# Feed-forward weights in steps of 1024 elements, in slots that stay through the whole kernel

## The chip, the cores and the metric

The kernel runs on one core of a Trainium2 chip. The metric is the device time of one execution in microseconds (us). Before the change the median of 3 runs is 1696.09 us (1696.07 to 1696.68).

## The reference

One layer of a streaming encoder on x of 256 rows (SEQ) by 2048 (D), all float32:

```
h      = RMSNorm(x) * attn_norm_g
proj   = h @ w_in                       # latents, rope key, diff q/k/v, gate logits
y_mla  = latent attention (16 heads),  y_diff = differential attention (8 heads)
merged = g0 * (y_mla @ w_mla_proj) + g1 * (y_diff @ w_diff_proj)
x      = x + merged @ w_out
h2     = RMSNorm(x) * ffn_norm_g
x      = x + (silu(h2 @ w_gate) * (h2 @ w_up)) @ w_down     # 2048 -> 5632 -> 2048
out    = RMSNorm(x) * final_norm_g
```

The change lies in the feed-forward part (the last three lines) and in the slots for weights that the part before it, here called the front, uses too.

## The kernel before

**Precision.** Every product of two float32 matrices is made of three matmuls. `split` (L89 to L97) makes of a tile a high part (ACT's cast to fp32r, L92) and a low part (DVE's difference of the tile and its high part, L93). `mm3` (L174 to L178) issues left high x right high (L176), left high x right low (L177) and left low x right high (L178) into one PSUM bank. The left operand is a 128x128 block of activations that TensorE loads, the right one a weight block of 128x512 that it streams. So each weight is loaded, cast by ACT, subtracted by DVE and then used by TensorE.

**Front (up to 945 us).** `weights` (L134) loads tiles of up to 128 x 2 x 512 into `raw` (6 slots of 4 KB a partition), high parts into `whi`, low parts into `wlo` (4 slots each). `project` and `project_t` use them; attention runs in between as generators that `advance` steps. All these slots lie in the pool `wp`, which is closed at the end of the front with the attention's pool `ap` and the front's PSUM pool `ps` (`front.close()`). The last product of the front is `w_out` (L586 to L607): its result plus x gives x2 (L593), which TensorE transposes (L601); ACT and DVE scale and split it (L95, L96) into `h2T`, 16 blocks of 128 x 256.

**Feed-forward.** Behind it two pools are opened, `fp` (SBUF) and `fq` (PSUM), on the memory that the front has left; each tile waits for the old tiles under it. `fp` holds `raw` (3 slots of 128 x 4 x 512, 8 KB a partition), `w` (5 such slots, for high and low parts and for sums) and `r` (2 slots of 128 x 3 x 512).

The 5632 hidden columns are 11 blocks of 512, in three `parts` of 4, 4 and 3. For each part `hidden(c, ...)` makes its blocks one after the other, and then the down projection adds their share to x2, in four column groups c of 512.

In `hidden` the 16 blocks of `h2T` go in 8 pairs. A pair needs four weight blocks from `w_gu`: u0, g0 (up and gate for the first block of the pair) and u1, g1 (for the second); one load of 1 MB brings them. A plain pair makes 2 halves of rows x 2 blocks x (gate, up) = 8 products, 24 matmuls, into the banks 2, 3, 4 and 8. Pairs 0, 2 and 4 (`SEVEN`) are done as a 2x2 block product by seven products, 21 matmuls, into banks 1 to 7. Their right sides are three loaded blocks (g0, g1, u1; parts in `r`) and four sums: T1 = g0 + u0, T3 = u1 + u0 (both L638), T2 = T1 + u1 (L639), T4 = T2 + g1 (L640); parts in `w`. The left sides are blocks of `h2T` and sums of them made in the front (`h2S`). Behind pair 4, DVE and ACT gather banks 1, 5, 6, 7 (L690 to L694); behind pair 7 they empty banks 2, 3, 4 and 8 and make silu(gate) * up (L714, L715, L717, L718). The result is transposed before pair 6 of the next block, or in the down projection (L668).

In the down projection each load of `w_fd` brings four blocks of 128 x 512 (a step m): 4 x 2 products, 24 matmuls; L753 adds a group's result to x2. The last column group of the last part has its weights split ahead into `L` tiles and is normalized and stored at once.

**Order.** Each engine runs its instructions in the order of the instruction stream. That order is set when the kernel is built: a scheduler goes through the program in order of priority (program order first) with estimated times and gives each engine, at each estimated moment, the first instruction that is ready and whose tiles have a slot. So instructions of later steps can stand ahead of earlier ones that were estimated to wait, on TensorE too. All weight loads are issued on SP's queue, each when a `raw` slot is free.

Of the kernel before, what the change touches and what calls it, by code (L numbers as in the profile page):

```python
# [8 lines left out]
F32 = mybir.dt.float32  # L9
# [5 lines left out]
P = 128  # L15
# [23 lines left out]
def hybrid_block(ctx: ExitStack, tc: tile.TileContext, x, xT, gains, w_lat, w_kr, w_dqk, w_dv, w_g0, w_g1, b_gate,  # L39
# [4 lines left out]
    up = ctx.enter_context(tc.tile_pool(name="up", bufs=1))  # L44
    st = ctx.enter_context(tc.tile_pool(name="st", bufs=1))
    dram = ctx.enter_context(tc.tile_pool(name="dram", bufs=1, space=bass.MemoryType.DRAM))

    front = ExitStack()
    wp = front.enter_context(tc.tile_pool(name="wp", bufs=1))
    ap = front.enter_context(tc.tile_pool(name="ap", bufs=1))  # L50
    ps = front.enter_context(tc.tile_pool(name="ps", bufs=1, space=bass.MemoryType.PSUM))

# [81 lines left out]
    def weights(w, c, g0=0, ng=None, cut=None, alloc=None):  # L134

        m, n = w.shape[3:]
        cut = cut or m
        full = [P, 1024 // n, n] if n == 256 else [P, 2, 512]
        res = []
        for g in range(g0, g0 + (ng or w.shape[1])):  # L140
            raw = wp.tile([P, m, n], F32, tag="raw", name=nm("raw"), bufs=6, padded_shape=full)
            if alloc is None:
                for i in range(0, m, cut):
                    nc.sync.dma_start(out=raw[:, i:i + cut], in_=w[c, g, :, i:i + cut])
                whi = wp.tile([P, m, n], F32R, tag="whi", name=nm("whi"), bufs=4, padded_shape=full)
                wlo = wp.tile([P, m, n], F32R, tag="wlo", name=nm("wlo"), bufs=4, padded_shape=full)
            else:
                nc.sync.dma_start(out=raw, in_=w[c, g])
            for i in range(0, m, cut):
                if alloc is None:  # L150
                    hi, lo = whi[:, i:i + cut], wlo[:, i:i + cut]
                else:
                    hi, lo = alloc(F32R, (P, cut, n)), alloc(F32R, (P, cut, n))
                split(raw[:, i:i + cut], hi, lo)
                res += [(hi[:, j], lo[:, j]) for j in range(cut)]
        return res
# [315 lines left out]
    t1 = []  # L472
# [147 lines left out]
        return fq.tile(list(shape), F32, tag=f"q{role}", name=nm("q"), bufs=1)  # L620

    def load(src):
        raw = fp.tile([P, 4, 512], F32, tag="raw", name=nm("raw"), bufs=3)
        nc.sync.dma_start(out=raw, in_=src)
        return raw

    def wide(dt=F32R):
        return fp.tile([P, 4, 512], dt, tag="w", name=nm("w"), bufs=5)

    def plain_weights(src):  # L630
        raw, hi, lo = load(src), wide(), wide()
        split(raw, hi, lo)
        return [(hi[:, j], lo[:, j]) for j in range(4)]

    def seven_weights(src):

        raw, t = load(src), wide(F32)
        nc.vector.tensor_tensor(out=t[:, 0:2], in0=raw[:, 1::2], in1=raw[:, 0:1].broadcast_to([P, 2, 512]), op=ALU.add)  # L638
        nc.vector.tensor_tensor(out=t[:, 2], in0=t[:, 0], in1=raw[:, 3], op=ALU.add)  # L639
        nc.vector.tensor_tensor(out=t[:, 3], in0=t[:, 2], in1=raw[:, 2], op=ALU.add)  # L640
        rh, rl = (fp.tile([P, 3, 512], F32R, tag="r", name=nm("r"), bufs=2) for _ in range(2))
        split(raw[:, 1:4], rh, rl)
        th, tl = wide(), wide()
        split(t, th, tl)
        return [(rh[:, j], rl[:, j]) for j in range(3)], [(th[:, j], tl[:, j]) for j in range(4)]

    def part_of(a, h):
        hs = slice(h * P, (h + 1) * P)
# [1 line left out]

    def seven_products(q, pair, w, start, stop):

        (b11, b21, b22), (t1, t3, t2, t4) = w
        hi, lo = h2S[pair]
        s1, s3, s2, s4 = [(hi[:, j], lo[:, j]) for j in range(4)]
        a0, a1 = h2T[2 * pair], h2T[2 * pair + 1]
        for i, l, r in ((1, part_of(a0, 0), b11), (5, s1, t1), (7, s3, t3), (6, s2, t2),
                        (2, part_of(a1, 0), b21), (3, s4, b22), (4, part_of(a1, 1), t4)):
            mm3(q[i], l, r, start, stop and i in (1, 5, 6, 7))

    def transposed(f, alloc=lt, roles=(5, 6)):

# [12 lines left out]
    def hidden(c, between):  # L675

        pairs = len(h2T) // 2
        last = max(SEVEN) if SEVEN else None
        q, base = {}, None
        for p in range(pairs):  # L680
            if p == pairs - 2:
                between()
            if p in SEVEN:
                w = seven_weights(w_gu[c, p])
                if not q:
                    q = {i: bank(i) for i in (1, 5, 7, 6, 2, 3, 4)}
                seven_products(q, p, w, p == min(SEVEN), p == last)
                if p == last:
                    c1, v2, v3, d12, d22 = (sc() for _ in range(5))
                    nc.scalar.copy(c1, q[1])  # L690
                    nc.vector.tensor_tensor(out=v2, in0=c1, in1=q[6], op=ALU.add)
                    nc.vector.tensor_tensor(out=d12, in0=q[5], in1=v2, op=ALU.subtract)
                    nc.vector.tensor_tensor(out=v3, in0=q[7], in1=v2, op=ALU.add)
                    nc.vector.tensor_tensor(out=d22, in0=q[5], in1=v3, op=ALU.subtract)  # L694
                    base = ((c1, d12), (v3, d22))
                continue
            u0, g0_, g1_, u1 = plain_weights(w_gu[c, p])
            if 8 not in q:
                q[8] = bank(8)
            if not SEVEN and not p:  # L700
                q.update({i: bank(i) for i in (2, 3, 4)})
            for a, (wg, wu) in ((h2T[2 * p], (g0_, u0)), (h2T[2 * p + 1], (g1_, u1))):
                first_k = a is h2T[0]
                for h, (i, j) in enumerate(((2, 3), (4, 8))):
                    l = part_of(a, h)
                    end = a is h2T[-1]
                    mm3(q[i], l, wg, first_k, end)
                    mm3(q[j], l, wu, first_k or (j == 8 and SEVEN and p == 1 and a is h2T[2]), end)
        f = []
        for h, (i, j) in enumerate(((2, 3), (4, 8))):  # L710
            sg = nt()
            gate, up_ = q[i], q[j]
            if base:
                nc.vector.tensor_tensor(out=sg, in0=base[h][0], in1=gate, op=ALU.add)  # L714
                nc.vector.tensor_tensor(out=base[h][1], in0=base[h][1], in1=up_, op=ALU.add)  # L715
                gate, up_ = sg, base[h][1]
            nc.scalar.activation(out=sg, in_=gate, func=AF.Silu, scale=r2[:, h:h + 1])  # L717
            nc.vector.scalar_tensor_tensor(out=sg, in0=up_, scalar=r2[:, h:h + 1], in1=sg, op0=ALU.mult, op1=ALU.mult)  # L718
            f.append(sg)
        return f  # L720
# [42 lines left out]
        nc.gpsimd.tensor_scalar(out=rest[:, h:h + 1], in0=s3, scalar1=D * EPS, scalar2=None, op0=ALU.add)  # L763
    ws = []
    for m in range(a, b):
        raw = load(w_fd[3, m])
        for j in range(4):
            ws.append((lt(F32R, (P, 512)), lt(F32R, (P, 512))))
            split(raw[:, j], ws[-1][0], ws[-1][1])
    for h in range(2):  # L770
        hs = slice(h * P, (h + 1) * P)
        z, y = x2[3][h], lt(shape=(P, 512))
# [56 lines left out]
def _arrays(inputs):  # L829

    import numpy as np

    a = {n: np.asarray(v) for n, v in inputs.items()}
    a["xT"] = a["x"][0].T.reshape(D // P, P, S).transpose(1, 0, 2)
    a["gains"] = np.concatenate([a[n][0].reshape(-1, P).T for n in
                                 ("attn_norm_g", "ffn_norm_g", "q_norm_g", "kv_norm_g")], axis=1)
    w = a["w_in"][0]
    a["w_lat"], a["w_kr"] = _tiles(w[:, :1024], 512), _tiles(w[:, 1024:O_DQ], 320)
    a["w_dqk"], a["w_dv"] = _tiles(w[:, O_DQ:O_DV], 256), _tiles(w[:, O_DV:O_G], 512)
    a["w_g0"], a["w_g1"] = _tiles(w[:, O_G:O_G + D], 256), _tiles(w[:, O_G + D:], 512)  # L840
    w = a["w_uq"][0].reshape(QR, NH, QK)
    a["w_qn"] = _tiles(w[:, :, :NOPE].reshape(QR, -1), 256)
    a["w_qr"] = _tiles(w[:, :, NOPE:].reshape(QR, -1), 512)
    w = a["w_ukv"][0].reshape(KVR, NH, NOPE + VD)
    a["w_kn"] = _tiles(w[:, :, :NOPE].reshape(KVR, -1), 256)
    a["w_v"] = _tiles(w[:, :, NOPE:].reshape(KVR, -1), 256)
    for n, src, cols in (("w_mla", "w_mla_proj", 512), ("w_diff", "w_diff_proj", 512), ("w_out", "w_out", 512)):
        a[n] = _tiles(a[src][0], cols)

    wg, wu = (a[n][0].reshape(D // (2 * P), 2, P, NF, 512).transpose(3, 0, 1, 2, 4)  # L850
              for n in ("w_ffn_gate", "w_ffn_up"))
    a["w_gu"] = np.stack([wu[:, :, 0], wg[:, :, 0], wg[:, :, 1], wu[:, :, 1]], axis=3)
    a["w_fd"] = a["w_ffn_down"][0].reshape(NF, 4, P, 4, 512).transpose(3, 0, 2, 1, 4)
    a["consts"] = _constants()
    return [(n, np.ascontiguousarray(a[n])) for n in _INS]
# [16 lines left out]
```

## Time and profile before

| | |
|---|---|
| Median of 3 runs | 1696.09 us |
| Profiled execution, own time | 1696.72 us |
| Its span in the profile | 1694.9 us |
| Mean granted TensorE clock | 0.997 |
| TensorE matmuls | 1659.5 us busy, 98% of the span, 8443 matmuls |
| TensorE weight loads | 1405.4 us, 83% |
| DVE (VectorE) | 1146.8 us, 68% |
| ACT (ScalarE) | 829.2 us, 49% |
| GpSimd | 27.5 us, 2% |
| Mean DMA rate | 191 GB/s, 323.61 MB in all |

Busy times are those of one execution, taken by the hardware profiler. Matmuls are pipelined and their ends are modelled: the busy time of TensorE contains overlaps, and the idle time shown before a matmul is counted from the modelled end of the one before it. Lines such as L93 are lines of the kernel; `w<-raw,w` means that tile `w` is written from tiles `raw` and `w`.

### The profile page before, as it was taken

The numbers are of one execution on the slowest core, as the hardware profiler recorded it, in microseconds if no ns is written. First come the engines' busy times: TensorE is split into PE (matmuls) and PEld (weight loads), VectorE is DVE, ScalarE is ACT, GpSimd is POOL, SyncE is SP. The second block draws the span as 40 slices with busy tenths as digits, with TensorE's granted clock in tenths as the row PEclk, the third lists the DMA queues.
The fourth block names the chain that finished last, engine by engine and source line by source line (L and its number), as shares of the span: only waits on it lengthen the run. The fifth ranks groups of instructions, "written<-read, shape, count | busy, mean of one in ns | idle before, by whom it ended". The sixth has DMA issues, their size and how long they took to land.

```text
span 1694.9 us, 21463 instructions
## 1 busy us (share of the span) xinstructions
PE 1659.5 (98%) x8443; PEld 1405.4 (83%) x8443; DVE 1146.8 (68%) x1328; ACT 829.2 (49%) x998; POOL 27.5 (2%) x49
## 2 busy tenths in 40 slices
PE   8999999999999999999999899999999999999998
PEld 6888888888888999998888677787887777887776
DVE  7676666665545766665566688874688874588765
ACT  6455454544444665664444355543355553345532
POOL 0000000010000000000000000000000000000010
PEclk9999999999999999999999999999999999999999
DMA  9655455465665554456655455554555554555553
GB/s 324 217 174 174 174 175 180 146 205 201 217 207 190 175 175 166 160 191 223 233 201 199 142 180 199 199 199 174 183 201 189 197 199 174 200 198 197 185 195 118
DMA packets 80118, 323.61 MB, mean 191 GB/s; under 512 B 8848, under 2 KB 14992, under 8 KB 63120
## 3 DMA queue, kind: packets, MB, share of 16 engines
q1 hardware_dynamic: 79872, 322.21, 54.7%
q8 instruction: 66, 1.08, 0.3%
q14 instruction: 36, 0.29, 0.1%
q10 hardware_dynamic: 144, 0.02, 0.0%
HBM read 315.91 MB, written 6.29 MB: 190 GB/s over the span
## 4 chain that ended last, share of the span: by engine, by line
PE 88%; DVE 7%; issue 2%; ACT 2%; DMA 0%; SPq 0%; ACTq 0%; POOL 0%; POOLq 0%; DVEq 0%
PE mm L177 12%; PE mm L176 12%; PE mm L178 12%; PE q L177 11%; PE q L178 11%; PE q L176 10%; PE mm L201 9%; PE mm L202 5%; DVE w L93 3%; DVE r L93 2%; ACT w L92 2%; PE ps L178 1%; PE ps L177 1%; PE ps L176 1%; DVE n L718 1%
## 5 line engine op out<-in xcount | busy, mean ns | idle before, releaser
L93 DVE TENSOR_TENSOR wlo<-raw,whi 128x1024 fp32r<-128x1024 f32 (+3 forms) x320 | 381.8, 1193 | 266.2 <-ACT whi L92 260.0
L92 ACT CAST whi<-raw 128x1024 fp32r<-128x1024 f32 (+3 forms) x320 | 328.9, 1028 | 347.9 <-PE mm L178 221.6
L176 PE MATMUL mm<-whi,L 128*128 128x512 f32 (+2 forms) x1080 | 385.3, 359 | 5.4 <-ACT whi L92 5.4
L177 PE MATMUL mm<-wlo,L 128*128 128x512 f32 (+2 forms) x1080 | 386.0, 358 | 0.5 <-DVE wlo L93 0.5
L178 PE MATMUL mm<-whi,L 128*128 128x512 f32 (+2 forms) x1080 | 384.8, 357 | 0.0
L177 PE MATMUL q<-w,L 128*128 128x512 f32 x900 | 353.6, 393 | 11.6 <-DVE w L93 11.5
L178 PE MATMUL q<-w,L 128*128 128x512 f32 x900 | 351.0, 391 | 0.0
L176 PE MATMUL q<-w,L 128*128 128x512 f32 x900 | 308.8, 391 | 0.8 <-ACT w L92 0.7
L92 ACT CAST w<-raw 128x2048 fp32r<-128x2048 f32 x96 | 183.3, 1914 | 173.5 <-PE q L178 108.2
L93 DVE TENSOR_TENSOR w<-raw,w 128x2048 fp32r<-128x2048 f32 x96 | 219.6, 2288 | 57.5 <-PE q L177 38.0
L201 PE MATMUL mm<-L,whi 128*128 128x512 f32 x672 | 239.6, 398 | 0.6 <-DVE n L211 0.6
L176 PEld LDWEIGHTS mm<-whi,L 128*128 128x128 f32 x1080 | 204.1, 189 | 33.8 <-ACT whi L92 5.9
L177 PEld LDWEIGHTS mm<-wlo,L 128*128 128x128 f32 x1080 | 204.1, 189 | 28.9 <-DVE wlo L93 1.5
L178 PEld LDWEIGHTS mm<-whi,L 128*128 128x128 f32 x1080 | 204.0, 189 | 28.3
L177 PEld LDWEIGHTS q<-w,L 128*128 128x128 f32 x900 | 168.9, 188 | 54.8 <-DVE w L93 19.8
L176 PEld LDWEIGHTS q<-w,L 128*128 128x128 f32 x900 | 168.2, 188 | 36.1 <-ACT w L92 2.0
L178 PEld LDWEIGHTS q<-w,L 128*128 128x128 f32 x900 | 169.0, 188 | 34.0
L202 PE MATMUL mm<-L,wlo 128*128 128x256 f32 x672 | 189.2, 282 | 0.0
L201 PEld LDWEIGHTS mm<-L,whi 128*128 128x128 f32 x672 | 126.2, 188 | 28.7 <-DVE n L211 0.9
L202 PEld LDWEIGHTS mm<-L,wlo 128*128 128x128 f32 x672 | 127.0, 189 | 0.6
L92 ACT CAST w<-w 128x2048 fp32r<-128x2048 f32 x33 | 63.0, 1910 | 112.9 <-DVE w L640 98.6
L93 DVE TENSOR_TENSOR w<-w,w 128x2048 fp32r<-128x2048 f32 x33 | 75.6, 2292 | 59.7 <-ACT w L92 55.6
(190 smaller groups left out, 1364.8 us busy)
## 6 DMA issues: line engine op xcount, KB each, us to landing
raw<-in_w_gu_dram SPq DMA_DIRECT2D x88, 1024.0 KB, 4.7
raw<-in_w_fd_dram SPq DMA_DIRECT2D x44, 1024.0 KB, 4.7
raw<-in_w_dqk_dram SPq DMA_DIRECT2D x64, 512.0 KB, 4.0
raw<-in_w_g_dram SPq DMA_DIRECT2D x64, 512.0 KB, 3.3
raw<-in_w_diff_dram SPq DMA_DIRECT2D x32, 512.0 KB, 3.3
raw<-in_w_mla_dram SPq DMA_DIRECT2D x32, 512.0 KB, 4.2
raw<-in_w_out_dram SPq DMA_DIRECT2D x32, 512.0 KB, 3.9
raw<-in_w_dv_dram SPq DMA_DIRECT2D x30, 512.0 KB, 3.2
```

Of the source, the lines that this page charges most:

```text
L92: nc.scalar.copy(hi, src)
L93: nc.vector.tensor_tensor(out=lo, in0=src, in1=hi.bitcast(F32), op=ALU.subtract)
L176: nc.tensor.matmul(o, lhsT=l[0], rhs=r[0], start=start, stop=False)
L177: nc.tensor.matmul(o, lhsT=l[0], rhs=r[1], start=False, stop=False)
L178: nc.tensor.matmul(o, lhsT=l[1], rhs=r[0], start=False, stop=stop)
L201: nc.tensor.matmul(o[b], lhsT=ws[k][0][:, bs], rhs=a, start=k == 0, stop=False)
L202: nc.tensor.matmul(o[b][:, :S], lhsT=ws[k][1][:, bs], rhs=ah, start=False, stop=k == len(aT) - 1)
L718: nc.vector.scalar_tensor_tensor(out=sg, in0=up_, scalar=r2[:, h:h + 1], in1=sg, op0=ALU.mult, op1=ALU.mult)
```

## The change

Weights of the feed-forward part move to the pool `wp`, which now stays open to the end of the kernel, in `raw` (6 slots) and `w` (8 slots), each of 128 x 2 x 512 (4 KB a partition). The front's `whi` and `wlo` become tiles of this `w`. Each load of 128 x 4 x 512 becomes two of 128 x 2 x 512, and each high or low part is made for 2 blocks at once. For a pair by seven products the sums and the parts of the loaded blocks go into five slots `t` of the pool `fp`; the parts of the sums go into `w`. The order of the four blocks in `w_gu` (set when the arrays are laid out on the host) becomes g0, u1, u0, g1, so that T1 and T3 are one sum of the first half with u0. In the second and third pair by seven products of a block, the products of loaded blocks (1, 3, 2) come first; in the first pair the order of products stays.

```diff
@@ pools
+    wp = ctx.enter_context(tc.tile_pool(name="wp", bufs=1))
     front = ExitStack()
-    wp = front.enter_context(tc.tile_pool(name="wp", bufs=1))
@@ weights()
-                whi = wp.tile([P, m, n], F32R, tag="whi", name=nm("whi"), bufs=4, padded_shape=full)
-                wlo = wp.tile([P, m, n], F32R, tag="wlo", name=nm("wlo"), bufs=4, padded_shape=full)
+                whi = wp.tile([P, m, n], F32R, tag="w", name=nm("whi"), bufs=8, padded_shape=full)
+                wlo = wp.tile([P, m, n], F32R, tag="w", name=nm("wlo"), bufs=8, padded_shape=full)
@@ feed-forward helpers
     def load(src):
-        raw = fp.tile([P, 4, 512], F32, tag="raw", name=nm("raw"), bufs=3)
+        raw = wp.tile([P, 2, 512], F32, tag="raw", name=nm("raw"), bufs=6)
         nc.sync.dma_start(out=raw, in_=src)
         return raw

-    def wide(dt=F32R):
-        return fp.tile([P, 4, 512], dt, tag="w", name=nm("w"), bufs=5)
+    def two():
+        return wp.tile([P, 2, 512], F32R, tag="w", name=nm("w"), bufs=8)
+
+    def extra(dt=F32R):
+        return fp.tile([P, 2, 512], dt, tag="t", name=nm("t"), bufs=5)
+
+    def parts_of(src, alloc):
+        hi, lo = alloc(), alloc()
+        split(src, hi, lo)
+        return [(hi[:, j], lo[:, j]) for j in range(2)]

     def plain_weights(src):
-        raw, hi, lo = load(src), wide(), wide()
-        split(raw, hi, lo)
-        return [(hi[:, j], lo[:, j]) for j in range(4)]
+        return [w for m in (0, 2) for w in parts_of(load(src[:, m:m + 2]), two)]

     def seven_weights(src):
-        raw, t = load(src), wide(F32)
-        nc.vector.tensor_tensor(out=t[:, 0:2], in0=raw[:, 1::2], in1=raw[:, 0:1].broadcast_to([P, 2, 512]), op=ALU.add)
-        nc.vector.tensor_tensor(out=t[:, 2], in0=t[:, 0], in1=raw[:, 3], op=ALU.add)
-        nc.vector.tensor_tensor(out=t[:, 3], in0=t[:, 2], in1=raw[:, 2], op=ALU.add)
-        rh, rl = (fp.tile([P, 3, 512], F32R, tag="r", name=nm("r"), bufs=2) for _ in range(2))
-        split(raw[:, 1:4], rh, rl)
-        th, tl = wide(), wide()
-        split(t, th, tl)
-        return [(rh[:, j], rl[:, j]) for j in range(3)], [(th[:, j], tl[:, j]) for j in range(4)]
+        a, b = load(src[:, 0:2]), load(src[:, 2:4])
+        t13, t24 = extra(F32), extra(F32)
+        nc.vector.tensor_tensor(out=t13, in0=a, in1=b[:, 0:1].broadcast_to([P, 2, 512]), op=ALU.add)
+        nc.vector.tensor_tensor(out=t24[:, 0], in0=t13[:, 0], in1=a[:, 1], op=ALU.add)
+        nc.vector.tensor_tensor(out=t24[:, 1], in0=t24[:, 0], in1=b[:, 1], op=ALU.add)
+        w = {}
+        w[1], w[3] = parts_of(a, extra)
+        b21 = extra()
+        split(b[:, 1], b21[:, 0], b21[:, 1])
+        w[2] = b21[:, 0], b21[:, 1]
+        w[5], w[7] = parts_of(t13, two)
+        w[6], w[4] = parts_of(t24, two)
+        return w
@@ seven_products()
-        for i, l, r in ((1, part_of(a0, 0), b11), (5, s1, t1), (7, s3, t3), (6, s2, t2),
-                        (2, part_of(a1, 0), b21), (3, s4, b22), (4, part_of(a1, 1), t4)):
-            mm3(q[i], l, r, start, stop and i in (1, 5, 6, 7))
+        ls = {1: part_of(a0, 0), 2: part_of(a1, 0), 3: s4, 4: part_of(a1, 1), 5: s1, 6: s2, 7: s3}
+        for i in (1, 5, 7, 6, 2, 3, 4) if start else (1, 3, 2, 5, 7, 6, 4):
+            mm3(q[i], ls[i], w[i], start, stop and i in (1, 5, 6, 7))
@@ hidden()
-            u0, g0_, g1_, u1 = plain_weights(w_gu[c, p])
+            g0_, u1, u0, g1_ = plain_weights(w_gu[c, p])
@@ last column group
-        raw = load(w_fd[3, m])
         for j in range(4):
+            if j % 2 == 0:
+                raw = load(w_fd[3, m][:, j:j + 2])
             ws.append((lt(F32R, (P, 512)), lt(F32R, (P, 512))))
-            split(raw[:, j], ws[-1][0], ws[-1][1])
+            split(raw[:, j % 2], ws[-1][0], ws[-1][1])
@@ arrays on the host
-    a["w_gu"] = np.stack([wu[:, :, 0], wg[:, :, 0], wg[:, :, 1], wu[:, :, 1]], axis=3)
+    a["w_gu"] = np.stack([wg[:, :, 0], wu[:, :, 1], wu[:, :, 0], wg[:, :, 1]], axis=3)
```

## Rows read from the trace of the kernel before

**Rows 1.** Busy table of the whole span: busy us, share, instructions.

```profile
PE 1659.5 (98%) x8443; PEld 1405.4 (83%) x8443; DVE 1146.8 (68%) x1328; ACT 829.2 (49%) x998; POOL 27.5 (2%) x49
```

**Rows 2.** Timeline of TensorE: start us, us from first start to last end, instructions, [idle before].

```profile
968.04 1.75 PE L176 MATMUL q<-w,L 128*128 128x512 f32 x7
...
1143.00 0.38 PE L668 MATMUL q<-ident,n 128*128 128x128 f32 x2
...
1148.26 0.60 PE L668 MATMUL q<-ident,n 128*128 128x128 f32 x4
...
1150.63 0.50 PE L177 MATMUL q<-w,L 128*128 128x512 f32 x1 [1.30 <-DVE w L93]
...
1320.49 1.07 PE L176 MATMUL q<-w,L 128*128 128x512 f32 x4
1322.04 0.50 PE L176 MATMUL q<-r,L 128*128 128x512 f32 x1 [0.48 <-ACT r L92]
```

**Rows 3.** TensorE's waits before 945 us: in total, times, longest us.

```profile
PE mm L176 <- ACT whi L92: 5.4, 2, 4.5
```

**Rows 4.** TensorE's waits from 945 us on.

```profile
PE q L177 <- DVE w L93: 11.5, 17, 1.3
PE q L176 <- ACT r L92: 7.6, 9, 4.0
```

**Rows 5.** Stretches: length, busy us (instructions) of PE, PEld, DVE, ACT, POOL, clock, DMA.

```profile
945.50:965.00 19.50, 14.11 (x50) 9.65 (x50) 16.53 (x21) 8.70 (x9) 1.07 (x3) 0.82 0.26 83
1308.25:1352.20 43.95, 43.07 (x192) 34.98 (x191) 37.82 (x33) 22.53 (x17) 0.00 (x0) 1.00 0.54 191
1142.50:1164.00 21.50, 19.02 (x85) 15.05 (x85) 9.84 (x8) 8.07 (x6) 0.00 (x0) 1.00 0.33 117
1222.00:1264.00 42.00, 42.00 (x187) 34.75 (x186) 34.58 (x27) 19.37 (x12) 0.00 (x0) 1.00 0.58 200
...
951.30:958.10 6.80, 6.19 (x14) 3.78 (x14) 4.83 (x5) 4.19 (x4) 0.00 (x0) 0.62 0.46 154
```

**Rows 6.** Timeline of DVE, ACT and TensorE at the entry of the feed-forward part.

```profile
945.02 1.37 DVE L593 TENSOR_TENSOR L<-n,mm 128x512 f32<-128x512 f32 x2 [7.45 <-PE mm L178]
...
947.03 0.47 ACT L95 ACTIVATE L<-ps,gT 128x256 fp32r<-128x256 f32 x1 [10.74 <-PE ps L601]
...
949.84 1.46 ACT L92 CAST r<-raw 128x1536 fp32r<-128x1536 f32 x1
...
951.36 1.65 PE L176 MATMUL q<-r,L 128*128 128x512 f32 x3 [4.04 <-ACT r L92]
```

**Rows 7.** Timeline of DVE at the boundary of two blocks.

```profile
1310.17 2.29 DVE L93 TENSOR_TENSOR w<-raw,w 128x2048 fp32r<-128x2048 f32 x1
1312.38 1.22 DVE L638 TENSOR_TENSOR w<-raw 128x1024 f32<-128x1024 f32 x1
1313.51 1.41 DVE L718 SCALAR_TENSOR_TENSOR n<-s,r,n 128x512 f32<-128x512 f32 x2
...
1319.96 2.29 DVE L93 TENSOR_TENSOR w<-w,w 128x2048 fp32r<-128x2048 f32 x1 [2.05 <-ACT w L92]
```

**Rows 8.** Groups of instructions by shape: busy us, mean ns of one, idle before.

```profile
L93 DVE TENSOR_TENSOR wlo<-raw,whi 128x1024 fp32r<-128x1024 f32 x292 | 357.1, 1223 | 240.1 <-ACT whi L92 234.0 <-PE ps L514 3.5 <-DMA raw<-in_w_mla_dram 1.5
L93 DVE TENSOR_TENSOR w<-raw,w 128x2048 fp32r<-128x2048 f32 x96 | 219.6, 2288 | 57.5 <-PE q L177 38.0 <-issue 12.9 <-PE q L178 3.5
L92 ACT CAST whi<-raw 128x1024 fp32r<-128x1024 f32 x292 | 307.2, 1052 | 316.1 <-PE mm L178 205.4 <-PE mm L201 44.0 <-issue 32.2
L93 DVE TENSOR_TENSOR r<-raw,r 128x1536 fp32r<-128x1536 f32 x33 | 57.8, 1751 | 3.9 <-ACT r L92 3.9
L639 DVE TENSOR_TENSOR w<-w,raw 128x512 f32<-128x512 f32 x33 | 22.6, 686 | 0.4
```

**Rows 9.** DMA issues: tile, count, KB each, median us from issue to landing.

```profile
raw<-in_w_gu_dram SPq DMA_DIRECT2D x88, 1024.0 KB, 4.7
...
raw<-in_w_dqk_dram SPq DMA_DIRECT2D x64, 512.0 KB, 4.0
raw<-in_w_g_dram SPq DMA_DIRECT2D x64, 512.0 KB, 3.3
```

More of the change, by code (lines that the diff above doesn't have):

```diff
@@ L651, in seven_products @@
     def seven_products(q, pair, w, start, stop):
-        (b11, b21, b22), (t1, t3, t2, t4) = w
         hi, lo = h2S[pair]
```

## The prediction

> **What bounds the kernel now.** I read the busy table first. It shows TensorE's matmul row at 98% [rows 1], but the length of a matmul there is modelled and matmuls overlap, so 98% does not say how much is lost. The distance from one matmul to the next does. A run of seven takes 1.75 us and a run of four 1.07 us, so a matmul of 512 columns costs (1.75 - 1.07) / 3 = 0.227 us; a 128-column transpose costs (0.60 - 0.38) / 2 = 0.11 us [rows 2]. Second I read who TensorE waited for. In the whole front (up to 945 us) its largest wait is 5.4 us, 4.5 of it one wait at the start of the kernel [rows 3]. Almost all else is in the feed-forward part: `q` matmuls waiting for DVE's `w` (17 times) and for ACT's `r` (9 times) [rows 4]. So the kernel is bound by TensorE's issue, and what can be won are the holes of the feed-forward part. The weights made by ACT (cast) and DVE (subtraction) come too late there.
>
> Third I sized the holes by stretches [rows 5], as length minus matmuls times spacing:
> - **Entry, 945.5 to 965**: 50 matmuls, 8 of them transposes. 42 x 0.227 + 8 x 0.11 = 10.4 us of work in 19.5: 9.1 us lost. In its middle the granted clock is 0.62 of full, a mix of the 2.4 and 1.2 GHz levels, after TensorE had been nearly idle.
> - **A block of `hidden` that follows another block, 1308.25 to 1352.2**: 3 x 21 + 5 x 24 = 183 matmuls and 8 transposes, 42.4 us of work in 43.95: 1.6 us lost. The 9 waits for `r` [rows 4] are one at the entry and eight such blocks: 8 x 1.6 = 12.8 us.
> - **A block that follows the down projection, 1222 to 1264**: 187 matmuls in 42.0 us with TensorE busy throughout; nothing lost. So pairs by seven products are not in themselves too dear for DVE.
> - **The start of a down projection, 1142.5 to 1164**: 77 + 8 matmuls, 18.4 us of work in 21.5: 3.1 us lost, three times (one for each entry of `parts`): 9.3 us.
>
> Together 31 us, 1.8% of the profiled execution's 1696.72 us. That is all the change can win, since it takes no matmul away: a pair by seven products keeps 21, a plain pair 24.
>
> **The change part by part.**
>
> *Slots kept through the kernel (entry).* Before the entry DVE sits idle 7.45 us and ACT 10.74 us [rows 6], though only TensorE's last products of `w_out` keep them from feed-forward weights: the new pool lies on the memory of the front's weights, so `t`, `r` and `w` come free as those do. The first `r` is cast at 949.84, and TensorE starts at 951.36. With `raw` and `w` kept and `t` on the memory of the attention's pool (long unused), the first pair's sums, its loaded halves and then T1 to T4 can be made while `w_out` still runs: sums 1.22 + 2 x 0.69, subtractions 3 x 1.22 + 0.69, some 6.9 us [rows 8], which fits the 7.45 us that DVE was idle. The first four products need banks that the front's `mm` tiles have left, so TensorE can start when the last transposes are issued, or before. The clock also has no long pause in which to fall. Of 9.1 us I take 8 as gained. Bounds: 0 (the order is as before and DVE gets to it late) to 9.
>
> *Steps of 1024 elements.* One subtraction of 2048 elements takes 2.29 us, two of 1024 take 2 x 1.22 = 2.45: +0.16. A pair by seven products had 1.22 + 2 x 0.69 for its sums and 1.75 + 2.29 for its subtractions, 6.64 us; it now has the same sums, three subtractions of 1.22 and one of 0.69: 6.95, +0.31 [rows 8]. So DVE's work in one block rises by 3 x 0.31 + 5 x 0.16 = 1.7 us, from 37.8 [rows 5] to 39.5 us, against 42.4 us of TensorE work. By starts instead of durations it is less: the sum of 1024 at 1312.38 is followed at 1313.51 [rows 7], 1.13 us and not 1.22. This costs TensorE nothing while DVE is below it, but the cover is thin: 2.9 us in a block. The Trainium skill ("Perfetto Trace Analysis", Optimizing Scalar/DVE Operations) gives about 60 ns of fixed access cost per DVE instruction on SBUF and advises grouping where the engine is saturated. Eleven more instructions would by that be about 0.7 us a block, an estimate from that page; the rows above give up to 1.7, and the sum goes by the rows. The same section says that breaking up instructions helps where an unsaturated engine makes bubbles elsewhere, and the next paragraph is where that must show.
>
> *Loaded blocks first (boundary of two blocks).* At 1310.0 DVE is through the four sums that empty the old block's banks. Before, it then made one plain subtraction (from 1310.17), the sum, two L718, `r`, two more sums, waited 2.05 us for the cast of the whole `w`, and subtracted until 1322.25 [rows 7]; the products of T waited for that, and the next pair's `r` with them [rows 2]. After, from 1310.0 by starts: plain 2 x 1.13, T1/T3 1.13, L718 1.33, T2 and T4 1.4, the half `a` 1.13 (done 1317.3), g1 0.7 (1318.0), T1/T3 1.13 (1319.1), T2/T4 1.2 (1320.3). TensorE reaches this pair at 1318.45 and does products 1, 3, 2 first, 9 x 0.227 = 2.04 us; it wants `a`'s low parts from 1318.7, g1's at about 1320.0, T1's at 1320.7 and T2's at 1322.1. Everything is ready 1.4 us or more ahead. ACT has no single cast of 1.9 us left in this chain: while DVE sums, it casts what is there, so the 2.05 us wait goes. The plain pair behind has its subtractions from 1320.3 to 1322.6 and is wanted at 1323.4: this is late next, with 0.8 us to spare. I take 10 of 12.8 us as gained; bounds 0 to 12.8, and below nothing if DVE becomes the bound (rivals).
>
> *Down projection.* A half step's slots come free 12 matmuls (2.7 us) before the step ends, and a half's subtraction takes 1.2 us instead of 2.29. The hole of 1.3 us before the low products at 1150.63 [rows 2] should mostly close: 7 of 9.3 us; bounds 0 to 9.3.
>
> *Loads.* 132 loads of 1 MB become 264 of 512 KB. The front already lives on 512 KB loads that land in 3.3 to 4.0 us against 4.7 for 1 MB [rows 9], one each 2.7 us of TensorE work, without TensorE waiting [rows 3]. Cost nothing. SP issues 132 more; behind them stand only the final gains and the stores. The front's whi and wlo now share eight slots instead of four each: taken as 0, bounds -1 to +15 us (a rival has it).
>
> *Sum.* 8 + 10 + 7 = 25 us: 1696.72 - 25 = 1671.7 for a profiled execution; the median of the runs shown is 0.6 us under it, so **1671 us**.
>
> **The rivals.**
>
> *DVE becomes the bound in the blocks.* For it: 39.5 us of busy time, and if the 5.5 us or so of waits for casts stay (2.05 us [rows 7] in most of three pairs), 45 us against 43.95 now. The boundaries then gain nothing or lose 1 us each (8 us), while entry and down projection still gain 15: 1682 to 1690. Against it: the casts no longer come in one piece behind the last sum.
>
> *The gains cancel* with new holes of the same size: 1693 to 1699.
>
> *Casts take the slots (slower).* Eight slots under one name serve high and low parts. If a cast of the next step takes a slot before the subtraction it precedes, that low part waits until the running pair ends, because in a plain gate/up pair both halves ([g0, u1], [u0, g1]) are read to the end. u0's low part is wanted 4 matmuls, 0.91 us, into the pair; made after the slot is free it is there after 1.22 us, or 1.05 + 1.22 = 2.27 if the cast is late too [rows 8]: 0.3 to 1.4 us in each of 55 plain pairs, 17 to 75 us, against 15 from the other places: 1698 to 1756, say 1715. It decides from 0.27 us a pair on. Against it: at the boundary the writers of the shared `w` slots come in the order of the program (plain, sums, T) [rows 7].
>
> *The halves of a load come one after the other.* Then 1 MB takes 2 x 3.3 = 6.6 us or more [rows 9] against 24 x 0.227 = 5.4 of TensorE: 132 x 1.2 = 158 us slower, 1830. Against it the front, where such loads overlap. The Trainium skill ("DMA: Bandwidth & Descriptors", Measured) asks for batches of 1 MiB or more and so speaks against the change; the trace does not bear it out, since TensorE waits for none of the 512 KB loads behind the start [rows 3].
>
> **How the numbers follow.** Forecast (1664 to 1681) 0.66; DVE bound 0.18; cancelled 0.05; slots 0.09; loads 0.02. Faster by over 0.2% (3.4 us, about what a measurement of this kernel can tell from no change) 0.84, within 0.05, slower 0.11. The range reaches from all 31 us and a little more won to the end of the second case: 1663 to 1690.
>
> **What would show it.** Right: no pause between the last `w_out` transposes and the first product of the entry, and granted clock 1.0 there; TensorE's waits for `r`/`t` and `w` down from some 20 us to under 6; a block after a block in 42.4 to 42.8 us; DVE's wait for ACT at T gone. Wrong: DVE at 40 us or more in a block with TensorE waiting for low parts (first rival); a short hole before the low products of every plain pair (slots); waits for `raw` (loads); or holes in the front, where now there are none.

## The result, and the profile after

The changed kernel takes 1665.55 us (median of 4 runs, 1665.15 to 1666.32) against 1696.38 us for the kernel before on the same chip: a ratio of 0.9818, 95% interval 0.9801 to 0.9835. That is 30.8 us, where 25 were forecast (1671 us, range 1663 to 1690). The span of the profiled execution fell from 1694.9 to 1663.6 us.

The waits of TensorE from 945 us on (each line: total us, times, longest us) are the first view, and the answer to [rows 4]: both kinds of wait for weights are gone, and what is left is three short waits at the entry, 2.3 us in all.

```profile
PE ps L601 <- DVE L L593: 2.0, 2, 1.8
PE q L176 <- DVE L L96: 0.3, 1, 0.3
```

The stretches of [rows 5], found by counting matmuls from the start, in the same order (length, then busy us and instructions of PE, PEld, DVE, ACT, POOL, granted clock, DMA share, GB/s):

```profile
944.81:958.00 13.19, 10.90 (x50) 8.54 (x50) 11.62 (x19) 6.19 (x9) 1.07 (x3) 1.00 0.36 117
1289.66:1331.88 42.22, 42.22 (x191) 34.94 (x190) 37.83 (x44) 23.22 (x28) 0.00 (x0) 1.00 0.62 199
1128.68:1147.03 18.35, 18.35 (x85) 15.25 (x84) 10.18 (x11) 8.32 (x9) 0.00 (x0) 1.00 0.56 186
1205.06:1246.99 41.93, 41.93 (x186) 34.72 (x185) 33.54 (x36) 20.45 (x23) 0.00 (x0) 1.00 0.62 199
```

The second one starts one matmul (0.23 us) later than the stretch of [rows 5]. Before the change the stretch between the same two matmuls reads:

```profile
1308.47:1352.21 43.74, 42.86 (x191) 34.79 (x190) 37.61 (x33) 22.32 (x17) 0.00 (x0) 1.00 0.54 192
```

The entry went from 19.50 to 13.19 us (-6.3, forecast -8), this block that follows a block from 43.74 to 42.22 (-1.5), the start of a down projection from 21.50 to 18.35 (-3.15). Counted in the same way at every place, the eight blocks that follow a block gained 1.5 to 2.4 us each, 14.0 together (forecast 10), the three down projections 9.0 (forecast 7), and the rest of the first block 1.0. That is 30.3 of the 31.3 us by which the profiled span fell; the remaining 1.0 lies before the entry and at the end. The fourth stretch, without a hole before, moved by 0.07. In both middle stretches PE's busy time equals the length: TensorE is at its spacing of 0.227 us and nothing is left there.

At the boundary of two blocks DVE's timeline reads (answers to [rows 7]; the new block's first matmul starts at 1289.44):

```profile
1292.77 2.35 DVE L93 TENSOR_TENSOR w<-raw,w 128x1024 fp32r<-128x1024 f32 x2
...
1295.71 1.21 DVE L93 TENSOR_TENSOR w<-t,w 128x1024 fp32r<-128x1024 f32 x1
1296.84 1.22 DVE L93 TENSOR_TENSOR t<-raw,t 128x1024 fp32r<-128x1024 f32 x1
1297.98 1.22 DVE L93 TENSOR_TENSOR w<-t,w 128x1024 fp32r<-128x1024 f32 x1
1299.11 0.68 DVE L93 TENSOR_TENSOR t<-raw,t 128x512 fp32r<-128x512 f32 x1
```

The low parts of T1 and T3 are done at 1296.9, those of T2 and T4 at 1299.2, the last loaded one at 1299.8. TensorE reaches this pair at 1299.6 (45 matmuls, 10.2 us, behind the block's first) and issues its first matmul with the low part of a loaded block at 1302.1. No row has a wait for a cast in front.

At the entry the rest shows:

```profile
946.07 1.27 DVE L593 TENSOR_TENSOR L<-n,mm 128x512 f32<-128x512 f32 x2
...
946.80 0.44 PE L601 MATMUL ps<-ident,L 128*128 128x128 f32 x2 [1.83 <-DVE L L593]
...
948.03 0.47 PE L176 MATMUL q<-t,L 128*128 128x512 f32 x1
```

The first product follows the last transpose directly (0.6 us from 947.39 to 948.03 for six of them) and the granted clock of the stretch is 1.00. But L593, which ran as soon as `w_out` was through [rows 6], now starts 1.1 us after it: a subtraction for the plain pair (L93, from 944.33) and a sum (L647, from 945.46) stand ahead of it on DVE.

### The profile page after: what moved, and what is told of

Its sections match the earlier page's. It is cut to its first block, busy times and chain, and to the rows that moved or that the text cites. A ratio compares the mean times of both kernels' runs of the same rounds, so it can differ in the third digit from the quotient of the medians.

```text
span 1663.6 us, 22367 instructions
## 1 busy us (share of the span) xinstructions
PE 1648.0 (99%) x8443; PEld 1407.1 (85%) x8443; DVE 1158.8 (70%) x1490; ACT 845.2 (51%) x1158; POOL 26.2 (2%) x49
## 4 chain that ended last, share of the span: by engine, by line
PE 97%; DMA 1%; DVE 1%; ACT 0%; issue 0%; SPq 0%; ACTq 0%; POOLq 0%; POOL 0%; DVEq 0%
PE q L176 14%; PE q L177 14%; PE q L178 14%; PE mm L176 12%; PE mm L177 12%; PE mm L178 12%; PE mm L201 9%; PE mm L202 5%; PE ps L178 1%; PE ps L177 1%; PE ps L176 1%; PE q L677 1%; PE ps L108 1%; DMA raw<-in_w_dqk_dram 1%; DMA raw<-in_w_gu_dram 0%
## 5 line engine op out<-in xcount | busy, mean ns | idle before, releaser
L93 DVE TENSOR_TENSOR wlo<-raw,whi 128x1024 fp32r<-128x1024 f32 (+3 forms) x320 | 381.8, 1194 | 258.1 <-ACT whi L92 252.8
L92 ACT CAST w<-raw 128x1024 fp32r<-128x1024 f32 x192 | 198.9, 1052 | 262.2 <-PE q L177 254.3
L93 DVE TENSOR_TENSOR w<-raw,w 128x1024 fp32r<-128x1024 f32 x192 | 231.7, 1220 | 108.7 <-ACT w L92 108.7
L93 DVE TENSOR_TENSOR w<-t,w 128x1024 fp32r<-128x1024 f32 x66 | 79.6, 1218 | 4.6 <-ACT w L92 4.0
L92 ACT CAST w<-t 128x1024 fp32r<-128x1024 f32 x66 | 68.5, 1051 | 25.2 <-PE q L177 12.6
```

The lines of the kernel that those rows point to most:

```text
L92: nc.scalar.copy(hi, src)
L93: nc.vector.tensor_tensor(out=lo, in0=src, in1=hi.bitcast(F32), op=ALU.subtract)
```

## The experiments

All times are medians; "before" ran on the same chip each time (1696.7 to 1697.2 us). The stretches of a block after a block lie between the same two matmuls as the 43.74 us before and the 42.22 us after, those of a down projection as the 21.50 and 18.35 us.

**1. The slots not kept (keep_undone).** `raw` and `w` of the feed-forward part come from `wf`, opened behind the front:

```diff
-    wp = ctx.enter_context(tc.tile_pool(name="wp", bufs=1))
+    wp = front.enter_context(tc.tile_pool(name="wp", bufs=1))
...
+    wf = ctx.enter_context(tc.tile_pool(name="wf", bufs=1, reuse_waits="tile"))
```

> The changed kernel, but the pool of raw and w slots is closed with the front and opened anew behind it on the same memory; t still lies on the attention's memory; steps of 1024 and the order of products as changed. Theory (three places, the kept slots close only the entry): T1 to T4 must wait for the last w_out products and then for ACT and DVE, so 3 to 7 us of the entry's gain go and nothing else: 1669 to 1673 us against 1665.5, with blocks that follow a block still at about 42.2 us. Rival (the place of t alone closes the entry, since the first product needs only t): within 1.5 us of the changed kernel, 1665 to 1667.

Measured: 1670.44 us, ratio 0.9843 (0.9827 to 0.9859), 4.9 us over the changed kernel. TensorE's waits from 940 us on (its lines are one lower here):

```profile
PE q L175 <- ACT w L91: 4.4, 1, 4.4
PE ps L600 <- DVE L L592: 0.2, 1, 0.2
```

One wait of 4.4 us for a weight, at the entry, and none elsewhere: the kept slots close the entry and only the entry. The place of `t` is not enough. Part of the cost is the clock: from 951.6 to 956.6 us, behind the wait, it is granted at 0.50, the 1.2 GHz level, and 12 matmuls take 5.0 us in place of 12 x 0.227 = 2.7.

**2. Steps of 1024 without the kept slots and without the new order (steps_alone).** Like experiment 1, with `raw` and `w` in `fp` beside `t`, `whi` and `wlo` apart in the front as before, and the order 1, 5, 7, 6, 2, 3, 4 throughout.

> The kernel before with loads, sums and parts in steps of 1024 in pools opened behind the front (raw, w and t there; whi and wlo apart as before), and the old order of products. Theory (steps of 1024 with finer slots close the boundaries and the down projections, the order is spare): only the entry's gain is missing, 6 to 9 us: 1671 to 1675 us, a block after a block at 42.2 to 42.6 us. Rival (the order of products closes the boundaries): eight boundaries of 1 us or more on top, 1680 to 1686 us, blocks at 43.2 to 44 us.

Measured: 1671.48 us, 0.9849 (0.9835 to 0.9864). The block that follows a block:

```profile
1295.29:1337.51 42.22, 42.22 (x191) 34.95 (x190) 37.73 (x43) 23.06 (x28) 0.00 (x0) 1.00 0.62 199
```

It takes the 42.22 us of the changed kernel without the new order.

**3 and 4. The order undone, and the order alone (order_undone, order_alone).**

```diff
-        for i in (1, 5, 7, 6, 2, 3, 4) if start else (1, 3, 2, 5, 7, 6, 4):
+        for i in (1, 5, 7, 6, 2, 3, 4):
```

> The changed kernel with the order of products 1, 5, 7, 6, 2, 3, 4 in all pairs by seven products. Theory (parts are ready ahead, the order is spare): T1's low part is then wanted 1.4 us earlier, at about the time it is ready: 1665.5 to 1668 us. Rival (the order decides): 16 pairs behind a boundary or between lose up to 1 us each at eight boundaries, 1673 to 1679 us.

Measured: 1667.05 us, 0.9824 (0.981 to 0.9839).

> The kernel before with only the order of products changed to 1, 3, 2, 5, 7, 6, 4 in the second and third pair by seven products. Theory (the late part is the whole cast and subtraction of the sums, 2048 elements, which the order moves by at most 1.4 us, and the scheduler had put the ready products ahead already): 1692 to 1697 us. Rival (the order closes the boundaries): 12.8 us gained, 1683 to 1686 us.

Measured: 1696.88 us, 0.9999 (0.999 to 1.0009). The block that follows a block, first with the order undone, then with the order alone:

```profile
1292.51:1334.73 42.22, 42.22 (x191) 34.94 (x190) 36.88 (x42) 22.98 (x28) 0.00 (x0) 1.00 0.58 197
```

```profile
1308.94:1352.69 43.75, 42.87 (x192) 34.78 (x190) 37.62 (x33) 22.32 (x17) 0.00 (x0) 1.00 0.54 192
```

The order neither opens nor closes a boundary: 42.22 us as in the changed kernel, 43.75 against 43.74 before. The 1.5 us between 1667.05 and 1665.55 are not the order's by anything that the runs show. In the profile they lie where the edit changes no order of products: at the entry, whose clock is granted at 0.69 from 949 to 953 us (0.8 us longer), and in the first pair of the second block (1.3 us with the plain pair behind it), where DVE waited 3.1 us for a load (0.8 us in the changed kernel) and then emptied the old block's banks late. The run of 1666.16 us, the only one of the four with a mean granted clock of 0.999, lies among the changed kernel's (1665.15 to 1666.32, all 0.999).

**5. Shorter instructions in the old slots (pieces_old_slots).** The kernel before with

```diff
-        split(raw, hi, lo)
+        for j in (0, 2):
+            split(raw[:, j:j + 2], hi[:, j:j + 2], lo[:, j:j + 2])
...
-        split(t, th, tl)
+        for j in (0, 2):
+            split(t[:, j:j + 2], th[:, j:j + 2], tl[:, j:j + 2])
```

> The kernel before with its slots (raw 3, w 5, r 2, of 2048 and 1536 elements), loads and order, but each cast and subtraction of a plain pair, of a step of the down projection and of T1 to T4 made in two instructions of 1024 elements. Theory (length of one instruction: the cast of T1 and T3 no longer waits for T2 and T4, and the first low parts are there 1.1 us earlier): boundaries lose some 0.6 instead of 1.6 us, down projections some 2 instead of 3.1 us: 1682 to 1689 us. Rival (slots: three large slots of w per pair hold the parts back until whole pairs are done, the length of an instruction does not matter): under 3 us gained, 1693 to 1698 us.

Measured: 1671.25 us, 0.9849 (0.9832 to 0.9865), better than the theory's own range (1682 to 1689): the length of the instruction does more than the theory gave it. Slots, loads, layout and order are those of before, and 25.5 of the 30.8 us are there. The start of a down projection and the block after a block:

```profile
1133.71:1152.39 18.68, 18.67 (x86) 15.18 (x85) 9.76 (x10) 7.69 (x9) 0.00 (x0) 1.00 0.54 188
1295.03:1337.25 42.22, 42.22 (x192) 34.95 (x191) 38.23 (x40) 22.72 (x24) 0.00 (x0) 1.00 0.58 199
```

**6. Only T1 to T4 in two instructions (pieces_sums_only).** The second half of that diff.

> The kernel before with only the cast and subtraction of T1 to T4 made in two instructions of 1024 elements; plain pairs and down projection stay at 2048. Theory (each hole belongs to the instruction that is late in it): boundaries close by most of their 12.8 us, down projections keep their 9.3 us, and the entry loses a little: 1680 to 1686 us. Rival (one long instruction anywhere delays what stands behind it on DVE, so that the plain ones of 2.29 us must be halved too): 4 us or less gained, 1692 to 1697 us.

Measured: 1680.79 us, 0.9905 (0.9889 to 0.9922): 16.4 us gained. The block after a block, and the start of a down projection:

```profile
1298.91:1341.18 42.27, 42.27 (x191) 34.95 (x190) 37.91 (x35) 22.07 (x20) 0.00 (x0) 1.00 0.56 199
1134.82:1156.27 21.45, 18.97 (x86) 15.05 (x84) 9.85 (x8) 8.09 (x6) 0.00 (x0) 1.00 0.34 116
```

This boundary is closed, the down projection as before (21.50): each hole belongs to the long instruction that is late in it.

**7. Two names for the slots (names_apart).** Four `whi` and four `wlo` in `wp`, in the front and behind it, instead of eight `w`.

> The changed kernel with its eight slots under two names, four for high parts and four for low ones, in the front and behind it. Theory (slots are taken in program order, so that one name or two is the same): 1664.5 to 1667.5 us. Rival (under one name casts take slots ahead of the subtractions before them and delay low parts): apart is faster by 1 us or more, at or under 1664 us.

Measured: 1666.90 us, 0.9824 (0.981 to 0.9839). TensorE's waits from 940 us on are the same two rows, 1.5 and 0.3 us. Two names are not faster, so nothing here shows a cast that takes a slot from a subtraction. The 1.35 us more come with two runs with a mean granted clock of 0.998 (1667.5 and 1667.7 us); the two at 0.999 took 1665.9 and 1666.3.

**8 and 9. More work for DVE (sum_twice, sum_thrice).** The sum of T1 and T3 is made three times, or twice with `range(2)`:

```diff
-        nc.vector.tensor_tensor(out=t13, in0=a, in1=b[:, 0:1].broadcast_to([P, 2, 512]), op=ALU.add)
+        for _ in range(3):
+            nc.vector.tensor_tensor(out=t13, in0=a, in1=b[:, 0:1].broadcast_to([P, 2, 512]), op=ALU.add)
```

> The changed kernel with the sum of T1 and T3 made three times over in each of the 33 pairs by seven products: 2 x 1.22 us more DVE work in each, 7.3 us in a block by durations, 6.8 us by starts. Prediction's count (DVE's cover in a block is TensorE's 42.2 us less the busy time, 37.8 us): DVE becomes the bound, each of eight blocks that follow a block is 2.5 us longer or more, 1685 to 1700 us. Rival count (instructions overlap by some 0.08 us, so that the 44 of a block take 34.3 us and not 37.8): the added work still fits, 1666 to 1673 us.

> The changed kernel with the sum of T1 and T3 made twice: 1.22 us more DVE work in each of 33 pairs, 3.7 us in a block. Count by busy time (37.8 + 3.7 = 41.5 us under TensorE's 42.2 us): 1665.5 to 1669 us. Rival count (DVE's waits for casts and loads, some 2 us in a block, belong to its cycle and leave no room): some 1.3 us in each of eight blocks, 1674 to 1680 us.

Measured: 1677.12 us with two sums (0.9882, 0.9867 to 0.9896) and 1701.66 us with three (1.003, 1.0019 to 1.0042). The block after a block with two, then with three:

```profile
1295.89:1339.21 43.32, 42.90 (x192) 34.71 (x190) 40.88 (x46) 23.23 (x28) 0.00 (x0) 1.00 0.58 191
```

```profile
1308.35:1355.43 47.08, 44.81 (x191) 34.24 (x190) 44.14 (x49) 22.59 (x28) 0.00 (x0) 1.00 0.53 177
```

In these blocks the first added sums cost 1.1 us, the second 3.8 (over the eight such blocks 0.5 to 1.5 us with two sums and 1.5 to 5.6 with three). DVE is busy 94% in both (40.88 / 43.32, 44.14 / 47.08), and almost all the rest is its own waits: 1.4 us for casts and 1.0 for a load with two sums, one load with three:

```profile
DVE t L646 <- DMA raw<-in_w_gu_dram: 2.6, 1, 2.6
```

So DVE sets the pace together with what it waits for, and not only at 100% busy. The first sums raised DVE's busy time by 3.05 us (37.83 to 40.88) and the block by 1.1: about 2 us of work still fitted into the changed kernel's block. With three sums the count by starts fell and the count by busy time held in kind (the time lies 1.7 us above its range); with two the count by busy time missed, since it took 100% for the limit, and the rival's number came out.

**10. Six slots (six_slots).** `bufs=6` for `w` in place of 8.

> The changed kernel with six slots of w instead of eight, in the front and behind it. Theory (a plain gate/up pair reads both halves to its end and so holds four slots; with two left, the second half of the next pair is cast and subtracted only when the pair is through): 1.05 + 1.22 - 0.91 = 1.4 us in each of 55 plain pairs, 75 us: 1715 to 1760 us, the front unchanged. Rival (eight slots are more than is needed, as TensorE's work of 5.4 us a pair covers 2.3 us of making): under 6 us, 1665 to 1671 us.

Measured: 1721.43 us, 1.0143 (1.0126 to 1.016). The block after a block is 47.60 us, and the top of TensorE's waits:

```profile
PE q L177 <- DVE w L93: 11.4, 29, 1.3
PE q L176 <- DVE n L723: 8.7, 7, 1.6
PE q L176 <- ACT w L92: 8.0, 9, 1.4
```

Two slots fewer cost 56 us, but not as the theory has it, 1.4 us in each plain pair and nothing in the front. Some 5 us are lost in the front. The two pairs at the start of this block take 7.7 and 6.7 us in place of 4.8 and 5.4, the fifth, sixth and eighth nothing more. At that start DVE waits for a load, and the work that empties the old block's banks (L723) stands behind it:

```profile
1326.57 1.23 DVE L645 TENSOR_TENSOR t<-raw,raw 128x1024 f32<-128x1024 f32 x1 [3.01 <-DMA raw<-in_w_gu_dram]
1327.71 0.68 DVE L723 TENSOR_TENSOR n<-s,q 128x512 f32<-128x512 f32 x1
```

TensorE then waits for L723 (1.07 us, at 1328.45). That the time fell into the theory's range is luck. Why six slots make the load late was not taken apart.

**11. The entry's rest, first try (adds_first).** With `x2_add` the last L593:

```diff
+    def behind_adds(c, p):
+        return tc.issue_after(x2_add.ins) if c == 0 and 0 < p < 3 else nullcontext()
...
+                with behind_adds(c, p):
                     w = seven_weights(w_gu[c, p])      # and the same around plain_weights
```

> The changed kernel with DVE's work for the second and third pair of the first block queued behind the last two additions of x2 (L593), which stood 1.05 us behind it in the changed kernel. Theory (L593 releases the last transposes, and TensorE stands still for that long): 1 us off the entry, 1664 to 1665.3 us, too little for the interval but visible as the start of L593 within 0.2 us of the last w_out product. Rival (the work that is queued back is then late for the second pair): no gain or up to 2 us slower, 1665.5 to 1667.5 us.

Measured: 1668.96 us, 0.9835 (0.982 to 0.9849). The theory fell, and the time is above the rival's range too. L593 starts at 944.95, as `w_out` ends, but the work queued behind it now comes ahead of the last L96, which TensorE's first plain pair waits for. (Its left operands were made earlier; by the code, what L96 frees is a PSUM bank.) TensorE's waits, and the stretch behind the long one:

```profile
PE q L176 <- DVE L L96: 3.2, 1, 3.2
```

```profile
954.50:960.40 5.90, 5.83 (x14) 4.63 (x15) 4.42 (x5) 2.85 (x4) 0.00 (x0) 0.52 0.17 51
```

After that wait 14 matmuls run at a granted clock of 0.52, nearly all at the 1.2 GHz level: 5.9 us for what takes 14 x 0.227 = 3.2. The wait costs nearly twice what its row says.

**12. The entry's rest, second try (sums_behind).** With `x2_part` the last L96 of the front, and only the second pair by seven products queued behind it:

```diff
+        return tc.issue_after(x2_part.ins) if c == 0 and p == 2 else nullcontext()
```

> The changed kernel with only DVE's work for the second pair by seven products of the first block queued behind the last L96 of the front; the plain pair between keeps its place. Theory (the entry's rest comes from feed-forward sums that stand ahead of L593 and so of L96 on DVE; both are then about 1 us earlier and nothing else is later): 1 us off the entry, L593 within 0.2 us of the last w_out product, 1663.5 to 1665.5 us with the clock at its upper level throughout. Rival (the sums are now late for the second pair by seven products, as the plain parts were late in the run before): a hole of 1 us or more at that pair, 1666 to 1669 us.

Measured: 1664.38 us (1664.33 to 1664.69), 0.9809 (0.9796 to 0.9823). TensorE's waits, DVE's L593, and the entry between the same matmuls as the 13.19 us above:

```profile
PE q L176 <- DVE L L96: 0.3, 1, 0.3
PE ps L601 <- DVE L L593: 0.2, 1, 0.2
```

```profile
944.85 1.36 DVE L593 TENSOR_TENSOR L<-n,mm 128x512 f32<-128x512 f32 x2
```

```profile
945.33:956.89 11.56, 10.91 (x50) 8.54 (x50) 9.36 (x17) 5.61 (x9) 1.07 (x3) 1.00 0.29 91
```

This is the fastest version: 1.2 us under the changed kernel. The intervals of the ratios overlap, so the times alone do not show it, though the runs of the two do not (1665.15 the lowest of the changed kernel). The trace shows the 1.8 us of wait at L601 gone and the entry 1.6 us shorter, with every later block and down projection as in the changed kernel.

## Why the prediction was right, and which of its reasons were not

**What bounds and what can be won: right.** 31 us of holes were counted, 30.8 were gained, and in the middle stretches TensorE is at its spacing. That the two agree so closely is partly luck: the boundaries were counted from one block at 1.6 us each, and others gained up to 2.4 (14.0 in all, not 12.8), while 2.8 of the 9.1 us at the entry stayed. The forecast took 25 of the 31 us, each hole as closed in part; boundaries and down projections closed whole. Those shares are the terms that were mis-sized.

**Entry: right in mechanism, 6.3 us for 8.** Experiment 1 shows that the kept `raw` and `w` are worth 4.9 us; the rest of the 6.3 is put down to the shorter steps (argued, not shown by a run of its own), since the entry gets 0.9 to 2.8 us shorter in experiments 1, 2, 5 and 6 too, which have shorter instructions and no kept slots. The granted clock does not fall in the changed kernel's profile, as forecast, though in that of order_undone it fell to 0.69 at the same place. What was not foreseen is that the work made early also stands ahead of the front's last additions; experiment 12 gets that back.

**Boundaries: 14.0 us for 10, above its bound of 12.8 for the reason just given; the reason for the gain half right.** The prediction named two causes, a chain without a single 1.9 us cast, and loaded products first. Experiments 2 to 4 and 6 show that the first is all of it. Splitting the cast and subtraction of T1 to T4 alone takes the block from 43.74 to 42.27 us (12.7 of the 14.0 us over the eight); the order alone leaves it at 43.75; the order undone leaves 42.22. The chain worked out for DVE was also too late, by 2.3 us at T2 and T4 counted from the block's first matmul: the sums of the next pair were made before and while the old block was emptied, so T's parts were complete before TensorE came to the pair, and there was nothing left for the order to bridge.

**Down projection: 9.0 us for 7, one of two reasons right.** The prediction named half slots that come free 2.7 us earlier, and a half's subtraction of 1.2 us in place of 2.29. Experiment 5 has the old slots and closes 2.8 of the 3.15 us; experiment 6, which leaves the 2.29 us subtractions whole, closes none. So it is the second reason, the length of the instruction in front of the first low product; the slots are left with some 0.3 us.

**DVE's added work: size and limit both wrong, the cover near by luck.** The prediction put 1.7 us of added busy time on a block and counted what was left up to 100% busy, 2.9 us, as cover. DVE's busy time in the stretch rose by 0.2 us (37.61 to 37.83). Over the whole kernel it rose by 12 us (1146.8 to 1158.8) for 162 more instructions, 0.07 us each, so 0.7 us a block, the other figure in the prediction, was the nearer one. By the count to 100% busy the cover would be 4.4 us; experiment 8 shows some 2. The two errors nearly cancel. The Trainium skill ("Perfetto Trace Analysis", Optimizing Scalar/DVE Operations) advises breaking up instructions where an engine that is not saturated makes bubbles on others; experiments 5 and 6 agree, with 25.5 us gained in experiment 5, where DVE is busy 38.23 of 42.22 us in a block (91%). No run here tests its advice to group where the engine is saturated.

**Loads: right.** They land in 4.6 and 4.1 us at half the size:

```profile
raw<-in_w_gu_dram SPq DMA_DIRECT2D x176, 512.0 KB, 4.6
raw<-in_w_fd_dram SPq DMA_DIRECT2D x88, 512.0 KB, 4.1
```

DVE now waits for some of them (before, ACT's casts of `r` did: 18.4 us, 8 times), TensorE for none:

```profile
DVE t L645 <- DMA raw<-in_w_gu_dram: 15.9, 16, 2.8
```

That is what is late next: these waits of up to 2.8 us use up part of DVE's cover, and in the profiles of order_undone and six_slots TensorE lost time behind waits of 3.1 and 3.0 us. The Trainium skill ("DMA: Bandwidth & Descriptors", Measured) asks for batches of 1 MiB or more to reach 75% of peak bandwidth, a rule from loads issued by GpSimd. The trace does not bear it out as a cost here: these loads, issued by SP, move 199 GB/s in a block, and no wait of TensorE in the changed kernel is for a weight.

**The rivals.** DVE as the bound is real, but begins some 2 us of work later than the changed kernel stands. Casts that take slots: no sign of it (experiment 7). The price worked out for a late slot (17 to 75 us) holds the 56 us of six slots only by luck, since these are lost elsewhere. The front's shared slots cost nothing that shows: TensorE needs 939.9 us from its first matmul to the last of `w_out`, and 939.9 to 941.4 in the runs that have the front of before.

What stays open is the 1.0 us of the gain before the entry and at the end, which lies within that spread, and why a load comes late at one boundary and not at another.

## What to carry to other kernels

When the engine that makes operands has time to spare but its consumer waits, look at how long the one instruction in front of the first use is: halving it in the same buffers brought 25 of 31 us here, the kept buffers most of the rest, and the new order nothing that the runs show. Check the cover of the maker before (its busy time against the consumer's) and count its own waits for loads and casts with its work: here it held its consumer up at 94% busy. Work that is made early, or that can wait for a load, must not stand ahead of the small operations that release the consumer on an engine that runs its instructions in order.

## What the runs showed of the hardware that was not expected

- DVE held a block up at 94% busy in two runs with different amounts of work (40.88 of 43.32 us and 44.14 of 47.08 us); its waits for casts and loads, 2.4 and 2.6 us, were nearly all the rest.
- Two subtractions of 1024 elements in place of one of 2048 cost DVE little: 0.07 us for each instruction more over the whole kernel.
- Waits of TensorE of 3.2 us (experiment 11), 4.0 us [rows 6] and 4.4 us (experiment 1) at the entry were followed by stretches at a granted clock of 0.52, 0.62 and 0.50. The length of the last wait did not decide it alone: behind one of 1.8 us the clock stayed at 1.00 in the changed kernel, behind one of 1.6 us it fell to 0.69 in order_undone. In experiment 11 the slow stretch cost 2.7 us on top of the wait.
